# GpSimd's subtractions of weight panels and memory parts, whole or in pieces of 256 columns

## The chip, the core and the metric

The kernel runs on one core of one Trainium2 chip. The time is the device time of one launch in microseconds. Five engines matter: TensorE (PE in the profile), whose weight loads are shown apart (PEld), VectorE (DVE), ScalarE (ACT), GpSimd (POOL) and SyncE (SP), which issues the weight DMAs. Each engine works through its own queue in order and waits for the others by semaphores.

## The reference, cut to what matters

The model is three transformer-like layers over 256 tokens of width 1024: a convolution layer, a layer of differential attention and a layer of mixed sparse attention, the first two each followed by a cross attention over 256 memory tokens, all three with a gated feed-forward block. Nearly all of the work is products of activations with weights that are used once:

```python
k = (mem @ w_k).reshape(B, M, MEM_HEADS, MEM_HEAD_DIM)
v = (mem @ w_v).reshape(B, M, MEM_HEADS, MEM_HEAD_DIM)
...
x = x + swiglu(rms_norm(x, norm_ffn[i]), ffn_w_gate[i], ffn_w_up[i], ffn_w_down[i])
```

All is float32. The kernel keeps the accuracy by splitting each operand a into a high part, which is a rounded to the format that TensorE multiplies in one pass, and a low part, a minus the high part. A product is then hi x hi + hi x lo + lo x hi. The change concerns the subtraction that makes the low parts.

## The kernel before, in words

The weights come as 382 panels of 128 rows and up to 1024 columns, listed in the order of use by `declare`. For each panel `load_to` issues a DMA from SyncE into a buffer `wf` (six of them), and `prep_to` makes the two parts in a ring of five buffers each: ScalarE copies `wf` to `whi` with rounding, and VectorE or GpSimd subtracts, `wlo = wf - whi` (line 278). Which of the two is set per group of panels by a table of letters, `LO`, that is repeated over the panels of the group: "gv" gives every other panel to GpSimd, "g" all of them, "v" none. All panels of the four products for memory K and V (`mk`, `mv`: 4 x 8 panels of 1024 columns) are GpSimd's.

`gemm` consumes panels in order and keeps five prepared ahead. For a panel with `nk` of 1 TensorE multiplies 128 columns of the panel at a time, three products for each, 24 matmuls of 256 columns for 1024 panel columns. A panel with `nk` of 2 or 4 holds several row blocks side by side, so one panel serves 2 or 4 steps. A matmul that reads `wlo` waits for the subtraction that wrote those columns.

Memory parts: the keys and values of the memory are split in the same manner after their product, in quarters of 512 columns (`mem_parts`, line 585): `memK0`, `memV0` and `memV1` on GpSimd, `memK1` on VectorE. The memory itself is split by `mem_split` (line 503), also on GpSimd, which isn't touched.

GpSimd has more in its queue between the panels: sums of squares for the norms (`sacc`, line 338), their folds (`sfold`, line 355), inverse square roots of a few numbers (`rr`, line 372; `orr`, line 918) and the gated products of the last block (`hf`, line 1391). VectorE has, beside its panels, the residuals and low parts of activations, the normalisation of the convolution (`lsq`, line 624), the scaling of attention (`p` in lines 708 and 890, `o` in line 923) and the masked minima (line 324), behind which ScalarE's exponentials `sp` follow. Engine order is fixed when the program is built; at run time only the waits decide.

Of the kernel before, what the change touches and what calls it, by code (L numbers as in the profile page):

```python
# [21 lines left out]
F32 = mybir.dt.float32  # L22
# [3 lines left out]
OP = mybir.AluOpType  # L26
# [157 lines left out]
def program(ctx: ExitStack, tc: tile.TileContext, A, out):  # L184
    nc = tc.nc
    V, SC, G, PE = nc.vector, nc.scalar, nc.gpsimd, nc.tensor
# [69 lines left out]
    def load_to(n):  # L256
        while state["dma"] < min(n, len(panels)):
            p = panels[state["dma"]]
            p["f"] = stage.tile([128, WMAX], F32, name="wf", tag="wf")
            nc.sync.dma_start(p["f"][:, :p["W"]], p["ap"])  # L260
            for f in state["loads"].get(state["dma"], []):
                f()
            state["dma"] += 1

    def prep_to(n):
        while state["prep"] < min(n, len(panels)):
            i = state["prep"]
            load_to(i + 1)
            p = panels[i]
            W = p["W"]  # L270
            p["hi"] = ring.tile([128, WMAX], F32R, name="whi", tag="whi")
            p["lo"] = ring.tile([128, WMAX], F32R, name="wlo", tag="wlo")
            with ExitStack() as late:
                for ins in state["after"]:
                    late.enter_context(tc.issue_after(ins.ins))
                p["ih"] = SC.activation(p["hi"][:, :W], p["f"][:, :W], AF.Copy)  # L276
                eng = G if p["eng"] == "g" else V
                p["il"] = eng.tensor_tensor(p["lo"][:, :W], p["f"][:, :W], p["hi"][:, :W].bitcast(F32), op=OP.subtract)  # L278
            state["prep"] += 1
            load_to(i + NS_PANEL)  # L280

    def consume():
        i = state["use"]
        prep_to(i + state["ahead"])
        state["use"] += 1
        return panels[i]
# [190 lines left out]
    for j in range(4):  # L477
        for c in (2 * j, 2 * j + 1):
            to_set(S0, c, x[:, c], vc("g_mix", c))
        prep_to(j + 1)  # L480
        st.add(x[:, 2 * j:2 * j + 2])
# [99 lines left out]
    def mem_parts(dst, src, n, act, after, eng=G):  # L581
        with tc.issue_after(act.ins):
            SC.activation(dst[0][:, n], src[:, n], AF.Copy)
        with tc.issue_after(after.ins):
            eng.tensor_tensor(dst[1][:, n], src[:, n], dst[0][:, n].bitcast(F32), op=OP.subtract)

    def split(dst, at, ps):
        SC.activation(dst[0][at], ps, AF.Copy)
# [53 lines left out]
    with tc.high_priority():  # L642
        rs = spread(st.r)
        for s in (slice(0, 1), slice(1, 2), slice(2, 4), slice(4, 6), slice(6, 8)):
# [7 lines left out]
    st = Stats()  # L652
    jobs = [(dst, src, n) for dst, src in ((memK[0], fK[0]), (memV[0], fV[0])) for n in range(4)]
    jobs = [lambda d=d, s=s, n=n: mem_parts([quarters(t) for t in d], quarters(s), n, LN["last"], LN["st"].ins) for d, s, n in jobs]
    gemm(8, S1, FM8, resid(st, [(S0, "g_mem", 0)], bias="b_pw2"), hooks={i: jobs[2 * i:2 * i + 2] for i in range(4)},
         tail=TAIL)
# [3 lines left out]
    def mem_attention(i, Sq, So, st, evac):  # L660
        with ExitStack() as es:
            P = es.enter_context(tc_pool(name=f"ma{i}", bufs=3))
            P1 = es.enter_context(tc_pool(name=f"mq{i}", bufs=1))
            if i:
                K = [P1.tile([128, NCH, S], F32R, name=f"memK1{p}") for p in "hl"]
                W = [P1.tile([128, 2, D], F32R, name=f"memV1{p}") for p in "hl"]
                later = [lambda n=n: mem_parts([quarters(t) for t in K], quarters(memK[1][0]), n, st.square, st.low, V)
                         for n in range(4)]
                later += [lambda n=n: mem_parts([quarters(t) for t in W], quarters(memV[1][0]), n, st.square, st.ins)
                          for n in range(4)]  # L670
            else:
                K, W, later = memK[0], memV[0], []
# [680 lines left out]
    gemm(4, [u[:, 4:8] for u in S1], TM4, evO, tail=TAIL)  # L1353
    state["ahead"], state["after"] = NB_PANEL, late[2:]
    prep_to(state["use"] + 4)
    state["after"] = []
    eb.close()
# [79 lines left out]
```

## Time and profile before

| what | value |
|---|---|
| median of 3 runs | 1178.34 us (1177.95 to 1182.44) |
| the profiled execution | 1176.31 us |
| its span (first to last instruction) | 1174.5 us |
| TensorE matmuls busy | 1121.0 us, 95% |
| VectorE busy | 787.4 us, 67% |
| ScalarE busy | 650.7 us, 55% |
| GpSimd busy | 425.3 us, 36% |
| panel subtractions on VectorE, all widths | 251, 319.0 us |
| panel subtractions on GpSimd, all widths | 131, 285.3 us |

[...] An engine that is idle costs nothing as long as no other waits for it.

### The profile page before, as it was taken

The numbers are of one execution on the slowest core, as the hardware profiler recorded it, in microseconds if no ns is written. First come the engines' busy times: TensorE is split into PE (matmuls) and PEld (weight loads), VectorE is DVE, ScalarE is ACT, GpSimd is POOL, SyncE is SP. The second block draws the span as 40 slices with busy tenths as digits, with TensorE's granted clock in tenths as the row PEclk, the third lists the DMA queues.
The fourth block names the chain that finished last, engine by engine and source line by source line (L and its number), as shares of the span: only waits on it lengthen the run. The fifth ranks groups of instructions, "written<-read, shape, count | busy, mean of one in ns | idle before, by whom it ended". The sixth has DMA issues, their size and how long they took to land.

```text
span 1174.5 us, 21545 instructions
## 1 busy us (share of the span) xinstructions
PE 1121.0 (95%) x8418; PEld 1061.5 (90%) x8418; DVE 787.4 (67%) x1445; ACT 650.7 (55%) x1141; POOL 425.3 (36%) x278
## 2 busy tenths in 40 slices
PE   7999989999999998988999999999889998999997
PEld 7998878999999998978999999999887677999986
DVE  6899856586766456666754565645758746888843
ACT  6565476565545354654756554535576645675642
POOL 5999846220000015773626444001554210111300
PEclk9999989999999999998999999999889998999999
DMA  7576534355546544542433654753645115454661
GB/s 259 194 248 211 186 116 170 108 164 188 190 144 232 184 148 145 193 132 84 133 119 129 216 193 143 236 183 105 209 162 163 36 55 163 160 196 155 224 197 37
DMA packets 59799, 191.13 MB, mean 163 GB/s; under 512 B 6752, under 2 KB 10080, under 8 KB 59696
## 3 DMA queue, kind: packets, MB, share of 16 engines
q1 hardware_dynamic: 58288, 187.31, 48.4%
q0 software_dynamic: 688, 1.90, 0.5%
q8 instruction: 66, 1.08, 0.4%
q10 hardware_dynamic: 720, 0.53, 0.1%
q14 instruction: 37, 0.30, 0.1%
HBM read 188.15 MB, written 1.05 MB: 161 GB/s over the span
## 4 chain that ended last, share of the span: by engine, by line
PE 44%; DVE 2%; issue 2%; POOL 1%; ACT 1%; POOLq 0%; DVEq 0%; ACTq 0%
PE acc L409 38%; PE acc L1116 1%; PE acc L1214 1%; DVE wlo L278 1%; POOL sacc L338 1%; PE acc L723 0%; PE acc L1275 0%; PE acc L1279 0%; PE aux L1256 0%; PE acc L1368 0%; POOL sfold L355 0%; PE acc L1276 0%; PE acc L1211 0%; PE acc L692 0%; POOL rmr L1320 0%
## 5 line engine op out<-in xcount | busy, mean ns | idle before, releaser
L276 ACT ACTIVATE whi<-wf 128x1024 fp32r<-128x1024 f32 (+3 forms) x382 | 370.9, 986 | 318.9 <-PE acc L409 277.0
L278 DVE TENSOR_TENSOR wlo<-wf,whi 128x1024 fp32r<-128x1024 f32 (+3 forms) x251 | 319.0, 1280 | 180.5 <-ACT whi L276 179.6
L278 POOL TENSOR_TENSOR wlo<-wf,whi 128x1024 fp32r<-128x1024 f32 (+1 forms) x131 | 285.3, 2194 | 183.5 <-ACT whi L276 183.3
L409 PE MATMUL acc<-s0h,whi 128*128 128x256 f32 x1192 | 340.5, 287 | 5.9 <-ACT whi L276 5.4
L409 PE MATMUL acc<-s0h,wlo 128*128 128x256 f32 x1192 | 338.2, 284 | 3.5 <-POOL wlo L278 3.5
L409 PE MATMUL acc<-s0l,whi 128*128 128x256 f32 x1192 | 337.6, 284 | 1.6 <-DVE s0l L435 1.6
L409 PEld LDWEIGHTS acc<-s0h,whi 128*128 128x128 f32 x1192 | 229.9, 193 | 7.2 <-ACT whi L276 5.4
L409 PEld LDWEIGHTS acc<-s0h,wlo 128*128 128x128 f32 x1192 | 229.1, 192 | 4.9 <-POOL wlo L278 4.6
L409 PEld LDWEIGHTS acc<-s0l,whi 128*128 128x128 f32 x1192 | 229.6, 193 | 1.9 <-DVE s0l L435 1.8
L409 PE MATMUL acc<-s1h,whi 128*128 128x256 f32 x736 | 205.9, 281 | 1.0 <-ACT s1h L649 1.0
L409 PE MATMUL acc<-s1h,wlo 128*128 128x256 f32 x736 | 205.5, 280 | 0.6 <-DVE wlo L278 0.3
L409 PE MATMUL acc<-s1l,whi 128*128 128x256 f32 x736 | 205.5, 280 | 0.3 <-DVE s1l L435 0.3
L409 PEld LDWEIGHTS acc<-s1h,whi 128*128 128x128 f32 x736 | 138.1, 188 | 1.7 <-ACT s1h L649 1.4
L409 PEld LDWEIGHTS acc<-s1h,wlo 128*128 128x128 f32 x736 | 138.3, 188 | 1.0 <-DVE wlo L278 0.5
L409 PEld LDWEIGHTS acc<-s1l,whi 128*128 128x128 f32 x736 | 138.4, 188 | 0.7 <-DVE s1l L435 0.5
L409 PE MATMUL acc<-hh,whi 128*128 128x256 f32 x352 | 99.6, 283 | 0.0
L409 PE MATMUL acc<-hl,whi 128*128 128x256 f32 x352 | 99.6, 283 | 0.0
L409 PE MATMUL acc<-hh,wlo 128*128 128x256 f32 x352 | 99.6, 283 | 0.0
L338 POOL TENSOR_TENSOR sacc<-sq,sacc 128x512 f32<-128x512 f32 x21 | 33.8, 1612 | 122.1 <-ACT sq L337 121.7
L543 DVE SCALAR_TENSOR_TENSOR aux<-u,vecs,aux 128x256 f32<-128x256 f32 x174 | 68.6, 476 | 1.2 <-ACT aux L541 1.2
L409 PEld LDWEIGHTS acc<-hl,whi 128*128 128x128 f32 x352 | 67.6, 192 | 0.0
L409 PEld LDWEIGHTS acc<-hh,wlo 128*128 128x128 f32 x352 | 67.6, 192 | 0.0
(371 smaller groups left out, 1724.6 us busy)
## 6 DMA issues: line engine op xcount, KB each, us to landing
wf<-in_gu SPq DMA_DIRECT2D x120, 512.0 KB, 3.9
wf<-in_w_down SPq DMA_DIRECT2D x66, 512.0 KB, 4.3
wf<-in_mem_w_k SPq DMA_DIRECT2D x16, 512.0 KB, 4.3
wf<-in_mem_w_v SPq DMA_DIRECT2D x16, 512.0 KB, 3.7
wf<-in_mem_w_q SPq DMA_DIRECT2D x16, 512.0 KB, 3.5
wf<-in_mem_w_o SPq DMA_DIRECT2D x16, 512.0 KB, 4.2
wf<-in_w_pw SPq DMA_DIRECT2D x24, 256.0 KB, 3.0
wf<-in_gv SPq DMA_DIRECT2D x24, 256.0 KB, 2.6
```

What stands on the lines that cost most here:

```text
L276: p["ih"] = SC.activation(p["hi"][:, :W], p["f"][:, :W], AF.Copy)
L278: p["il"] = eng.tensor_tensor(p["lo"][:, :W], p["f"][:, :W], p["hi"][:, :W].bitcast(F32), op=OP.subtract)
L338: self.ins = self.eng.tensor_tensor(self.acc, sq, self.acc, op=OP.add)
L409: PE.matmul(o, l, r, start=(ki == 0 and n == 0 and q == 0), stop=(ki == K - 1 and q == 2), skip_group_check=True)
L543: V.scalar_tensor_tensor(cv[:, c] if k == TAPS - 1 else ai, src, w, ai, op0=OP.mult, op1=OP.add)
L1116: PE.matmul(ph[0:60, 0:256], win[:, a, 4 * g + j], w[:, j * 256:(j + 1) * 256], start=(g == 0 and j == 0 and w is p["hi"]), stop=(g == 3 a ...
L1214: PE.matmul(f, q1, kk[:, kv], start=True, stop=True, skip_group_check=True)
```

## The change

Where GpSimd makes a low part, the instruction over the whole width becomes one instruction for each 256 columns: four for a panel of 1024, two for 512, four for 816 (three of 256 and one of 48), two for a quarter of a memory part. VectorE's subtractions stay whole.

```diff
-                eng = G if p["eng"] == "g" else V
-                p["il"] = eng.tensor_tensor(p["lo"][:, :W], p["f"][:, :W], p["hi"][:, :W].bitcast(F32), op=OP.subtract)
+
+                eng, step = (G, 256) if p["eng"] == "g" else (V, W)
+                for c in range(0, W, step):
+                    w = slice(c, min(c + step, W))
+                    p["il"] = eng.tensor_tensor(p["lo"][:, w], p["f"][:, w], p["hi"][:, w].bitcast(F32), op=OP.subtract)
...
         with tc.issue_after(after.ins):
-            eng.tensor_tensor(dst[1][:, n], src[:, n], dst[0][:, n].bitcast(F32), op=OP.subtract)
+            for c in range(0, 512, 256 if eng is G else 512):
+                w = slice(c, c + (256 if eng is G else 512))
+                eng.tensor_tensor(dst[1][:, n, w], src[:, n, w], dst[0][:, n, w].bitcast(F32), op=OP.subtract)
```

The order of instructions on TensorE, VectorE, ScalarE and SyncE stays what it was; GpSimd's has 343 instructions more, and only one panel is taken apart by another instruction. Lines after the edit are 3 to 5 higher than before (278 becomes 281, 338 becomes 341, 918 becomes 923).

That place is the end of the first down projection and the differential attention behind it. GpSimd's queue there before (`sacc` and `sfold` are the norm's sums, `k` is a buffer filled with zeros, `orr` an inverse square root of the attention; x14 counts equal rows):

```order
L827 MEMSET k 64x8x256
L338 TENSOR_TENSOR sacc<-sq,sacc 128x512 x2
L278 TENSOR_TENSOR wlo<-wf,whi 128x1024
L338 TENSOR_TENSOR sacc<-sq,sacc 128x512
L355 TENSOR_TENSOR sfold<-sacc 128x256
L372 TENSOR_TENSOR rr<-ms,mhalf 128x2
L278 TENSOR_TENSOR wlo<-wf,whi 128x1024 x14
L918 TENSOR_TENSOR orr<-oms,mhalf 128x4
L278 TENSOR_TENSOR wlo<-wf,whi 128x1024 x4
```

and now:

```order
L832 MEMSET k 64x8x256
L341 TENSOR_TENSOR sacc<-sq,sacc 128x512 x2
L281 TENSOR_TENSOR wlo<-wf,whi 128x256 x3
L341 TENSOR_TENSOR sacc<-sq,sacc 128x512
L281 TENSOR_TENSOR wlo<-wf,whi 128x256
L358 TENSOR_TENSOR sfold<-sacc 128x256
L375 TENSOR_TENSOR rr<-ms,mhalf 128x2
L281 TENSOR_TENSOR wlo<-wf,whi 128x256 x56
L923 TENSOR_TENSOR orr<-oms,mhalf 128x4
L281 TENSOR_TENSOR wlo<-wf,whi 128x256 x16
```

The last piece of the first panel has moved behind the last `sacc`, ahead of `sfold`; the other panels are four pieces each in the same place.

On TensorE the matmuls stand where they stood, and what moved is a wait. This is the second query product of the first memory attention, whose panel (`whi_2114`, `wlo_2115`) serves four steps of 256 columns, before:

```order
L409 MATMUL acc_2335<-s0h_79,wlo_2115 128x256 [waits Pool_49]
L409 MATMUL acc_2335<-s0h_79,whi_2114 128x256
L409 MATMUL acc_2335<-s0l_80,whi_2114 128x256
L409 MATMUL acc_2335<-s0h_79,wlo_2115 128x256
L409 MATMUL acc_2335<-s0h_79,whi_2114 128x256
L409 MATMUL acc_2335<-s0l_80,whi_2114 128x256
L409 MATMUL acc_2335<-s0h_79,wlo_2115 128x256
```

and now (the same panel is `whi_2261`, `wlo_2262`):

```order
L412 MATMUL acc_2485<-s0h_79,wlo_2262 128x256 [waits Pool_49]
L412 MATMUL acc_2485<-s0h_79,whi_2261 128x256
L412 MATMUL acc_2485<-s0l_80,whi_2261 128x256
L412 MATMUL acc_2485<-s0h_79,wlo_2262 128x256
L412 MATMUL acc_2485<-s0h_79,whi_2261 128x256
L412 MATMUL acc_2485<-s0l_80,whi_2261 128x256
L412 MATMUL acc_2485<-s0h_79,wlo_2262 128x256 [waits Pool_49]
```

The first wait is now for one piece, and the step that reads the next 256 columns has a wait of its own.

## Rows read from the trace of the kernel before

**Rows 1.** The page, busy us of each engine, share of the span, instructions

```profile
PE 1121.0 (95%) x8418; PEld 1061.5 (90%) x8418; DVE 787.4 (67%) x1445; ACT 650.7 (55%) x1141; POOL 425.3 (36%) x278
```

**Rows 2.** Waits of TensorE: waiter, releaser, total us, times, longest us

```profile
PE aux L361 <- POOL sfold L355: 10.5, 7, 2.9
...
PE acc L926 <- DVE o L923: 4.4, 3, 2.0
PE acc L409 <- POOL wlo L278: 3.8, 6, 1.0
...
PE acc L1214 <- ACT sp L1173: 2.9, 1, 2.9
PE aux L712 <- DVE p L708: 2.3, 1, 2.3
...
PE aux L895 <- DVE p L890: 1.9, 1, 1.9
PE aux L630 <- DVE lsq L624: 1.7, 1, 1.7
```

**Rows 3.** Timeline of GpSimd, memory K and V: start us, us, instruction

```profile
115.05 0.64 POOL L612 TENSOR_TENSOR csum<-u,csum 128x256 f32<-128x256 f32 x1
115.65 2.41 POOL L278 TENSOR_TENSOR wlo<-wf,whi 128x1024 fp32r<-128x1024 f32 x1
118.01 0.74 POOL L612 TENSOR_TENSOR csum<-u,csum 128x256 f32<-128x256 f32 x1
118.71 4.77 POOL L278 TENSOR_TENSOR wlo<-wf,whi 128x1024 fp32r<-128x1024 f32 x2
```

**Rows 4.** Chain of waits, second feed-forward block: start us, us, what

```profile
648.17 169.78 PE acc L409 x1440
```

**Rows 5.** Timelines of VectorE and GpSimd, 886 to 899

```profile
888.31 1.20 DVE L278 TENSOR_TENSOR wlo<-wf,whi 128x1024 fp32r<-128x1024 f32 x1
...
890.03 6.08 DVE L278 TENSOR_TENSOR wlo<-wf,whi 128x1024 fp32r<-128x1024 f32 x2
...
888.75 6.29 POOL L278 TENSOR_TENSOR wlo<-wf,whi 128x1024 fp32r<-128x1024 f32 x2 [2.36 <-ACT whi L276]
```

**Rows 6.** Timelines of VectorE and GpSimd, 518 to 530

```profile
521.41 2.94 DVE L923 TENSOR_TENSOR o<-o,orr 128x256 f32<-128x256 f32 x2
...
524.46 2.11 DVE L888 SCALAR_TENSOR_TENSOR dcc<-dcc,lamc,dsm 128x2 f32<-128x2 f32 x1
...
521.24 2.49 POOL L278 TENSOR_TENSOR wlo<-wf,whi 128x1024 fp32r<-128x1024 f32 x1 [0.34 <-ACT whi L276]
524.04 2.52 POOL L278 TENSOR_TENSOR wlo<-wf,whi 128x1024 fp32r<-128x1024 f32 x1 [0.31 <-ACT whi L276]
```

**Rows 7.** Timelines of VectorE and GpSimd, 541 to 552

```profile
543.29 2.33 DVE L919 TENSOR_TENSOR orr<-orr,r 128x4 f32<-128x4 f32 x1 [1.12 <-POOL orr L918]
545.65 2.91 DVE L923 TENSOR_TENSOR o<-o,orr 128x256 f32<-128x256 f32 x2
...
543.22 2.38 POOL L278 TENSOR_TENSOR wlo<-wf,whi 128x1024 fp32r<-128x1024 f32 x1
```

**Rows 8.** Waits of TensorE, 541 to 552

```profile
PE acc L926 <- DVE o L923: 3.1, 2, 2.0
```

**Rows 9.** Timelines of VectorE and GpSimd, 584 to 593

```profile
587.89 2.40 DVE L708 TENSOR_SCALAR p<-p,sm 128x256 f32<-128x256 f32 x2
...
587.52 2.35 POOL L278 TENSOR_TENSOR wlo<-wf,whi 128x1024 fp32r<-128x1024 f32 x1
```

**Rows 10.** Timelines of VectorE and GpSimd, 145 to 202

```profile
147.73 3.26 DVE L624 TENSOR_TENSOR lsq<-lsq 128x512 f32<-128x512 f32 x2 [0.60 <-ACT lsq L622]
...
147.25 2.39 POOL L278 TENSOR_TENSOR wlo<-wf,whi 128x1024 fp32r<-128x1024 f32 x1 [1.69 <-ACT whi L276]
```

**Rows 11.** Timelines of VectorE and GpSimd, 56 to 63

```profile
57.31 2.88 DVE L553 SCALAR_TENSOR_TENSOR u<-t,vecs,sg 128x256 f32<-128x256 f32 x1 [4.66 <-ACT sg L552]
...
54.99 4.91 POOL L278 TENSOR_TENSOR wlo<-wf,whi 128x512 fp32r<-128x512 f32 x3
```

## The prediction

> **What bounds the kernel now.** I read the busy times first. TensorE's matmuls cover 95% of the span and GpSimd only 36% [rows 1], so GpSimd's own busy time is not the limit; the reader should see there that only what TensorE waits for can be won. The second view is therefore the list of TensorE's waits [rows 2]. Its largest entry, `sfold`, comes behind GpSimd sums of squares that the change leaves whole. Six others lead to the low halves: 3.8 us straight for `wlo` of GpSimd, and 4.4, 2.9, 2.3, 1.9 and 1.7 us behind VectorE operations (`o`, the mask chain before `sp`, two kinds of `p`, `lsq`). Together 17.0 us; that is the most which the change can reach by these waits.
>
> The third view, the timelines of VectorE and GpSimd at those five places, shows why VectorE is late there. Two panel subtractions that follow each other take 6.08 us, where the one just before took 1.20 [rows 5]; a GpSimd panel lies across each. Two multiplications `o` take 2.94 us, and a 128x2 operation 2.11 us, each ending as a GpSimd panel ends [rows 6]. So a VectorE operation with two inputs in SBUF stands still until GpSimd's current instruction is done, and a GpSimd instruction is a whole panel of 1024 columns, 2.36 us (the distance of the starts 115.65 and 118.01 in [rows 3]). The reverse is there too: GpSimd's two panels beside the 6.08 us take 6.29 instead of two times 2.36 [rows 5].
>
> [...]
>
> **What a piece costs GpSimd.** The trace has no subtraction of 256 columns. The nearest rows are additions of 256 columns with the next instruction right behind: starts 115.05 to 115.65 and 118.01 to 118.71, so 0.60 and 0.70 us [rows 3]. Four pieces take 2.40 to 2.80 us against 2.36 whole. I take 0.65, so 2.60. The edit adds 99x3 + 31 + 3 + 12 = 343 instructions; at 0.01 to 0.11 us more per piece GpSimd works 5 to 50 us longer over the whole span, nearly all of it in its idle 64%. The one place without idle time is the stretch of memory K and V, 32 panels that are all GpSimd's. TensorE takes 169.78 / 1440 x 24 = 2.83 us per panel [rows 4], so 2.60 keeps ahead by 0.23 and 2.80 just keeps up. The cover ends at 2.83 / 4 = 0.71 us per piece.
>
> [...]
>
> **The terms, each by this rule: VectorE now waits for the rest of one piece, runs, lets one piece pass, and runs again.** That GpSimd gets in between two VectorE operations is what [rows 5] show.
> - *Mask chain near 890* [rows 5]. GpSimd's panel can start at 889.5, when the 1.20 us subtraction ends. First piece to 890.15, subtraction to 891.35, piece to 892.0, subtraction to 893.2, where it was 896.1. That is 2.9 sooner, the whole of TensorE's wait of 2.9. The exponentials behind follow at their own pace; I take **2.5** (bounds 0 and 2.9).
> - *`o` and `p` near 521* [rows 6]. Waiting lasted from 521.41 to 523.73, so the pair itself needs 0.62. New: piece to 521.9, 0.31, piece 0.65, 0.31, so 523.2 instead of 524.35. The 128x2 operation then waits at most one piece, to about 524.1 instead of 526.6, but each of the two operations for `p` behind it can also pay a piece. Bounds 0 and 3.2 (1.9 for `p`, and 4.4 - 3.1 = 1.3 for `o`, the rest being the next term's); I take **1.6**.
> - *`o` near 545* [rows 7]. `orr` waited out a panel, and the pair `o`, 0.62 alone, was done at 548.56. New: piece to 543.87, 0.16, piece 0.65, 0.31, piece 0.65, 0.31, done near 546.0. TensorE waits 3.1 there [rows 8]; **2.5** (bounds 0 and 3.1).
> - *`p` near 588* [rows 9]. The pair took 2.40, of which 1.98 was waiting (to 587.52 + 2.35). New: 0.28 + 0.21 + 0.65 + 0.21 = 1.35, so 1.05 sooner, less 0.25 because four memory parts ahead of it in GpSimd's queue become eight pieces: **0.8** (bounds -0.3 and 2.3).
> - *`lsq` near 148* [rows 10]. 3.26 us for two additions, 1.91 of it waiting. New: 0.17 + 0.68 + 0.65 + 0.68 = 2.18: **1.1** (bounds 0 and 1.7).
> - *TensorE's own waits for `wlo`* [rows 2]. Matmuls now wait for the piece whose columns they read, so the first comes 0.6 to 1.8 us earlier. But where GpSimd works without a break, as before the first 1024-column panel [rows 11], a late panel makes the next one late, so only the last wait of a row counts, and slower pieces take some back: **0.6** (bounds -3 and 3.8).
> - *One reordered panel.* Near the end of the first down projection three pieces go ahead of the last sum of squares and the fourth between it and `sfold`. The work before `sfold` is the same: **-0.2** (0 to -0.4, by 0.60 to 0.70 per piece).
>
> Added waits: 226 more of TensorE's matmuls test a semaphore, nearly always one already passed because panels are prepared five ahead. The extra tests of ScalarE and SyncE name their own earlier `whi`, which is over. I cost them at nothing; the uncovered case is in the second rival.
>
> Sum: 2.5 + 1.6 + 2.5 + 0.8 + 1.1 + 0.6 - 0.2 = 8.9 us. The profiled execution took 1176.31 us (span 1174.5 and 1.8 around it), so 1167.4; it lies 2.0 under the median of 1178.34, and with that the forecast is **1169 us**, its own range 1163 to 1173.
>
> **The rivals.**
> 1. *VectorE does not get in between pieces.* If GpSimd's next piece is in hand when one ends, VectorE waits for the whole panel as before. For it: near 57 an operation took 2.88 us because two GpSimd subtractions that stood in a row passed ahead of it, up to 54.99 + 4.91 = 59.90 [rows 11]. Against: in [rows 5] VectorE got in between two GpSimd panels that stood back to back. Then only the 0.6 and -0.2 are left: 1178.
> 2. *GpSimd pays back.* The same lock lets VectorE hold up every piece, so a panel can lose 1.2 us up to four times instead of once, and chains of short VectorE operations pay a piece each time. If the terms for `o`, `p` and `lsq` come at half (-3.0) and the `wlo` term at -1.4 (-2.0): 8.9 - 5.0 = 3.9, 1174. For it: the 6.29 us in [rows 5]. Against: at the five places VectorE has few two-input operations per panel.
> 3. *Slower: GpSimd becomes the bound in memory K and V.* From 0.71 us per piece TensorE waits in each of the 32 panels. At 0.85 us it is 32 x (3.40 - 2.83) = 18.2 us, and 18.2 - 8.9 = 9.3 more than before: 1188. For it: that stretch leaves GpSimd 0.47 us per panel now (2.83 - 2.36). Against: 0.60 and 0.70 in [rows 3], with that very subtraction next in the queue.
>
> **How the numbers follow.** Within 0.5% is 1172.4 to 1184.2, about what a measurement here can tell from no change. The forecast gets 0.70, rival 1 0.14, rival 2 0.09, rival 3 0.07. Faster is the forecast, 0.70; the same is rivals 1 and 2, 0.23; slower is rival 3, 0.07. For eight in ten, the range goes from 1161 (all 17.0 us gone: 1178.3 - 17.0) to 1179, which takes in rivals 1 and 2.
>
> **What would show it.** Right: VectorE's panel subtractions beside GpSimd stay under 2 us; the pair near 890 ends about 3 us sooner; TensorE's waits for `o`, `sp` and both `p` fall from 11.5 (4.4 + 2.9 + 2.3 + 1.9) to under 5; the mean of GpSimd's pieces is below 0.9 us. Wrong: VectorE operations of 2.4 us remain (rival 1); GpSimd's pieces average over 1 us and new waits for `wlo` or `sfold` appear (rival 2); starts of uncontended pieces lie over 0.71 us apart and TensorE waits for `wlo` between 65 and 140 us (rival 3).

## The result and the profile after

The changed kernel is slower: 1191.72 us (four runs, 1187.17 to 1199.57) beside 1178.14 of the kernel before on the same chip, a ratio of 1.0127 with a 95% interval of 1.0108 to 1.0147. The forecast was 1169. The profiled execution took 1187.17 us (span 1185.4), 10.9 more than that of before. It is the fastest of the four, so what the others lost beyond that has no trace.

Three moments that both traces have show where this lies. TensorE spreads the layer norm's `rr` (L381) at 167.0 us, before at 154.5: 12.5 us are lost until there. Its first transposes of the differential attention stand at 511.9 and 490.7: 8.7 more are lost between. The last matmul ends at 1179.4 and 1168.5, so 10.4 are won behind it. The sum is 12.5 + 8.7 - 10.4 = 10.8. Time was won where four of the forecast's terms lie, and two losses that it did not have were larger.

The first lines are the page's busy times and TensorE's waits after the change (total us, times, longest).

```profile
PE 1120.9 (95%) x8418; PEld 1058.0 (89%) x8418; DVE 792.7 (67%) x1445; ACT 651.9 (55%) x1141; POOL 484.2 (41%) x621
...
PE aux L635 <- DVE lsq L629: 8.6, 1, 8.6
PE acc L412 <- POOL wlo L281: 5.2, 10, 1.2
...
PE acc L412 <- DVE s0l L438: 5.0, 1, 5.0
...
PE aux L900 <- DVE p L895: 4.1, 3, 2.9
...
PE acc L931 <- DVE o L928: 1.6, 2, 1.2
...
PE aux L717 <- DVE p L713: 1.3, 2, 0.9
```

TensorE is as busy as in [rows 1]. Against [rows 2] the wait for `o` fell from 4.4 to 1.6 us, for `p` of the memory attention from 2.3 to 1.3, that for `sp` is gone. `lsq` rose from 1.7 to 8.6, `s0l` from 1.6 to 5.0, and of the 4.1 for `p` L895 a single 2.9 is new. The next lines are the timelines of VectorE and GpSimd at these places. In what follows, a run is a row of GpSimd instructions without idle time between them (a line with a count can be the part of a run in the stretch shown); VectorE is held while a run passes ahead of an operation that it has begun, and gets in when that operation is done between two instructions of the run.

```profile
58.13 7.10 DVE L556 SCALAR_TENSOR_TENSOR u<-t,vecs,sg 128x256 f32<-128x256 f32 x1 [4.75 <-ACT sg L555]
...
56.47 8.47 POOL L281 TENSOR_TENSOR wlo<-wf,whi 128x256 fp32r<-128x256 f32 x12
...
66.58 30.79 POOL L281 TENSOR_TENSOR wlo<-wf,whi 128x256 fp32r<-128x256 f32 x44
...
151.73 11.37 DVE L629 TENSOR_TENSOR lsq<-lsq 128x512 f32<-128x512 f32 x3
...
150.49 12.06 POOL L281 TENSOR_TENSOR wlo<-wf,whi 128x256 fp32r<-128x256 f32 x16
...
198.10 6.37 DVE L281 TENSOR_TENSOR wlo<-wf,whi 128x1024 fp32r<-128x1024 f32 x1
...
197.80 5.59 POOL L281 TENSOR_TENSOR wlo<-wf,whi 128x256 fp32r<-128x256 f32 x8
...
500.53 10.96 DVE L893 SCALAR_TENSOR_TENSOR dcc<-dcc,lamc,dsm 128x2 f32<-128x2 f32 x1
...
499.63 11.84 POOL L281 TENSOR_TENSOR wlo<-wf,whi 128x256 fp32r<-128x256 f32 x17
...
542.99 1.83 DVE L928 TENSOR_TENSOR o<-o,orr 128x256 f32<-128x256 f32 x2
...
562.01 0.69 DVE L924 TENSOR_TENSOR orr<-orr,r 128x4 f32<-128x4 f32 x1 [1.12 <-POOL orr L923]
562.74 1.80 DVE L928 TENSOR_TENSOR o<-o,orr 128x256 f32<-128x256 f32 x2
...
604.76 1.25 DVE L713 TENSOR_SCALAR p<-p,sm 128x256 f32<-128x256 f32 x2
...
895.87 1.26 DVE L281 TENSOR_TENSOR wlo<-wf,whi 128x1024 fp32r<-128x1024 f32 x1
...
893.12 7.45 POOL L281 TENSOR_TENSOR wlo<-wf,whi 128x256 fp32r<-128x256 f32 x9 [0.86 <-ACT whi L276]
```

The lower rows are the forecast's rule at work: a pair of `o` 1.83 and 1.80 us where [rows 6, 7] had 2.94 and 2.91, `orr` 0.69 for 2.33, `p` 1.25 for 2.40 [rows 9], a panel subtraction of the mask chain 1.26 where a pair had 6.08 [rows 5]. The upper rows break it. `dcc`, 128x2 elements, takes 10.96 us and ends at 511.49, just behind the last of 17 pieces (499.63 + 11.84 = 511.47); sixteen pieces passed ahead of it. `wlo` took 6.37 us behind 8 pieces, the first `lsq` 9.1 of its 11.37 behind 13, `u` 7.10 where [rows 11] had 2.88. They came at the 25th (`dcc`), 22nd, 77th and 37th instruction of runs of 40, 29, 91 and 46; before that `wlo` VectorE had got in three times, and the `wlo` came at the 17th instruction after the last of these. So VectorE waits not for a piece but for what is left of the run; only `lsq`, done at 160.83, got in two pieces before the end of its run at 162.55. And 44 pieces in 30.79 us are 0.70 us each, the upper bound taken from [rows 3], 2.80 us a panel.

### The profile page after: what moved, and what is told of

It reads as the page before. It is cut to its first block, busy times and chain, and to the rows that moved or that the text cites. A ratio compares the mean times of both kernels' runs of the same rounds, so it can differ in the third digit from the quotient of the medians.

```text
span 1185.4 us, 21970 instructions
## 1 busy us (share of the span) xinstructions
PE 1120.9 (95%) x8418; PEld 1058.0 (89%) x8418; DVE 792.7 (67%) x1445; ACT 651.9 (55%) x1141; POOL 484.2 (41%) x621
## 4 chain that ended last, share of the span: by engine, by line
PE 43%; POOL 3%; issue 2%; DVE 1%; ACT 1%; POOLq 0%; DVEq 0%; ACTq 0%
PE acc L412 36%; POOL wlo L281 1%; PE acc L1121 1%; POOL sacc L341 1%; PE acc L1219 1%; PE acc L728 0%; PE acc L1280 0%; PE acc L1284 0%; POOL sfold L358 0%; PE aux L1261 0%; PE acc L1373 0%; PE acc L1281 0%; PE acc L1216 0%; PE acc L1202 0%; PE acc L697 0%
## 5 line engine op out<-in xcount | busy, mean ns | idle before, releaser
L281 DVE TENSOR_TENSOR wlo<-wf,whi 128x1024 fp32r<-128x1024 f32 (+3 forms) x251 | 309.9, 1244 | 188.2 <-ACT whi L276 179.1
L281 POOL TENSOR_TENSOR wlo<-wf,whi 128x256 fp32r<-128x256 f32 x462 | 345.0, 789 | 146.0 <-ACT whi L276 145.7
```

The source lines that it names most:

```text
L281: p["il"] = eng.tensor_tensor(p["lo"][:, w], p["f"][:, w], p["hi"][:, w].bitcast(F32), op=OP.subtract)
```

## Experiments

**Where the loss and the gain lie.** `"h"` stands for GpSimd in pieces of 256, `"g"` for whole panels; memory parts are whole in the first two kernels and in that of 512 columns.

```diff
 # e1: pieces from w_o on (and K, V, q, pw1, mq, mo as before)
-o="g", mq1="gvv", mo1="vgv", gu1="gv", T="vvg", cmp="ggv", w="gv", gv2="vgv"
+o="h", mq1="hvv", mo1="vhv", gu1="hv", T="vvh", cmp="hhv", w="hv", gv2="vhv"
 # e2: pieces in these alone
-pw1s="gv", pw1="g", mk="g", mv="g"
+pw1s="hv", pw1="h", mk="h", mv="h"
 # e4: everywhere, but two pieces a panel
-eng, step = (G, 256) ...
+eng, step = (G, 512) ...
```

> Pieces only for the panels of w_o, of the second memory attention and of what follows; every earlier GpSimd panel and every memory part whole again. Theory A (a VectorE instruction with two SBUF operands waits until a whole run of consecutive GpSimd pieces is through; the 10.9 us come from the long runs before 205 us and at 500 us): the long waits (lsq 9.1, wlo 6.4, dcc 11.0 us) are gone and the gains near 545, 588 and 890 us stay, so about 1178.2 - 6 = 1172 us, between 1169 and 1176. Theory B (a piece costs GpSimd 0.70 us and makes it the bound of memory K and V): also below before, 1170 to 1176, since K and V are whole. Theory C (more instructions and semaphores cost time everywhere): half of the pieces are left, so above 1178, near 1183.

Measured: 1167.34 us, ratio 0.9906 (0.9891 to 0.9921), faster than A and B allowed, so it does not tell them apart. Theory C falls: 132 of the 343 new GpSimd instructions (410 in all, before 278) are left, and the kernel is 10.5 us faster than the one before.

> Pieces only for the panels of w_pw1 and of memory K and V (before 160 us) and for the memory parts; all others whole as before. Theory A: the lsq addition near 151 us waits some 9 us again, the first u of a group some 7; 1178.2 + 8 = 1186 us, between 1183 and 1190. Theory B: TensorE's weight waits in 60 to 160 us are there in any case, but they sum to some 5 us; 1183 us with the wait at 151 us no part of it. Theory C: a quarter to a half of the whole loss, 1181 to 1184.

Measured: 1196.36 us (1189.23 to 1204.21), ratio 1.0157 (1.0117 to 1.0196), more than any theory gave. The profile has the `lsq` wait (7.9 us of TensorE) and one that the profile of the changed kernel did not have: `u` at 39.55 us takes 24.16 us, until a run of 42 instructions is through, and TensorE stands still for 12.9. The same operation at 38.97 us of the changed kernel got in, at the 12th instruction of GpSimd's run; here it was held from the 11th on. So the long wait can miss one execution and strike another. That this makes the scatter of the changed kernel's runs is not shown, as only the fastest has a trace.

> GpSimd takes panels in pieces of 512 columns (two for 1024), memory parts whole (512). A piece of 512 was spaced 1.25 us, so a panel costs GpSimd 2.5 us against TensorE's 2.83. Theory A: GpSimd catches up and stops for the next panel, the runs are short, the lsq addition waits under 4 us; the gains are about half of those of 256 columns; 1174 to 1180 us. Theory B: GpSimd is no bound, 1174 to 1178 us. A time above 1184 would speak against both.

Measured: 1173.22 us, ratio 0.9963 (0.9949 to 0.9978). That is 0.8 us below what A and B gave. The first `lsq` took 4.73 us, to the end of a run of 47 instructions, not under 4: GpSimd did not stop for each panel.

**One of VectorE's operands in PSUM.**

```diff
 # e3: first tile in PSUM, last sum in SBUF
-LN[j] = tmp.tile([128, 2, S], F32, name="lsq", tag="sq" if j else "sacc")
+LN[j] = tmp.tile([128, 2, S], F32, name="lsq", tag="sq") if j else b2(aux())
...
-V.tensor_tensor(LN[0], LN[0], LN[j], op=OP.add)
+V.tensor_tensor(to, LN[j], LN[0], op=OP.add)
 # e10: e3 and
-sg = poolC.tile([128, S], F32, name="sg", tag="sg")
+sg = ps[:, S:2 * S]
 # e6: e1 with the edit of e3; e11: e1 with both
```

> All pieces as in the changed kernel, but the sum of squares of the layer norm is kept in PSUM, so that each of its three VectorE additions near 151 us reads one operand from SBUF and one from PSUM instead of two from SBUF (the last writes SBUF). The pieces and their cost stay. Theory A: the u - mean subtractions, which read SBUF and PSUM, ran at 0.64 us each in the middle of the same run of pieces, so the additions run at once (under 1 us each), TensorE's wait at 154 us falls from 8.7 to under 2 us, and the time by 6 to 8 us against the changed kernel, to about 1184. Theory B: the wait is GpSimd's backlog, the weights come no sooner, the time changes by under 2 us (1190 to 1192).

Measured: 1195.81 us, ratio 1.0155 (1.0139 to 1.0171): no gain, and yet not what B said either. TensorE's waits and the timelines of VectorE and GpSimd of this kernel:

```profile
PE acc L412 <- DVE t L553: 12.7, 1, 12.7
...
PE aux L381 <- POOL rr L375: 9.1, 2, 7.0
```

```profile
38.70 23.33 DVE L556 SCALAR_TENSOR_TENSOR u<-t,vecs,sg 128x256 f32<-128x256 f32 x1 [0.18 <-ACT sg L555]
...
164.47 0.69 DVE L630 TENSOR_TENSOR aux<-lsq,aux 128x512 f32<-128x512 f32 x1
...
166.65 0.69 DVE L630 TENSOR_TENSOR lsum<-lsq,aux 128x512 f32<-128x512 f32 x1
...
163.26 11.10 POOL L281 TENSOR_TENSOR wlo<-wf,whi 128x256 fp32r<-128x256 f32 x16
174.29 1.74 POOL L375 TENSOR_TENSOR rr<-ms,mhalf 128x2 f32<-128x2 f32 x1
```

The additions run in 0.69 us in the middle of the pieces, as A said. But the next link, `rr`, is GpSimd's own and stands in its queue behind the same pieces: it starts at 174.29, and TensorE waits 7.0 us for it. Near 150 to 175 us GpSimd's backlog costs TensorE 7.0 us with the hold of `lsq` gone. The long wait of `u` is here too, so this time says nothing on what the hold of `lsq` alone cost; e13 below does.

> Pieces everywhere as in the changed kernel, the layer norm's sum of squares in PSUM, and the sigmoid of the gated unit written to PSUM too, so that neither the additions near 151 us nor the products u near 39, 58 and 91 us read two operands from SBUF. GpSimd's pieces cost the same. Theory A: of the waits before 165 us (TensorE stood still 12.9 us at 61 us in the kernel with the sum in PSUM alone) none over 2 us is left; what is left are the waits of wlo near 169 and 205 us and of the mask operation near 510 us, some 14 us of TensorE; 1195.8 - 12.9 = 1183 us, between 1179 and 1187. Theory B (GpSimd's cost of 0.70 us a piece is the bound there): no change, 1192 to 1197.

Measured: 1204.38 us (1195.12 to 1211.88), ratio 1.0235 (1.0196 to 1.0274). Both expectations missed. The products `u` no longer wait, but a VectorE operation over 128x64 (`lsc`) right behind one waits 20.66 us, and TensorE stands still for 9.2 us at 108 us, behind a `whi`.

> The kernel with pieces only in the panels of w_o and later (1167.3 us) and, with it, the layer norm's sum of squares kept in PSUM. Panels are whole where the additions run. Theory A: the additions no longer wait for a panel, TensorE's wait for the sums near 150 us (1.9 us) falls under 0.6; 1165.5 to 1166.5 us. If the wait only moves to the next VectorE operation, as it did with pieces everywhere: 1167.

Measured: 1164.85 us, ratio 0.9882 (0.9864 to 0.9900), 0.7 below A's range: `lsq` is out of TensorE's waits.

> Pieces only in the panels of w_o and later, with both the sum of squares and the sigmoid in PSUM: the candidate for the best version. Panels are whole where the products u run; they waited up to 3 us for a panel, but TensorE waited under 1 us behind them. Theory A: 1163 to 1165 us, 0 to 1.5 below the kernel with the sum alone (1164.9).

Measured: two groups, 1160.59 and 1163.22, and 1182.43, 1182.88 and 1183.80; the ratio, 0.9872 (0.9846 to 0.9897), is that of the lower group. The median of all five, 1182.43, is above the kernel before on that chip (1176.75), so A missed, and this version can't be called better. The profile is one of the upper, and its timeline shows what happens there, with whole panels:

```profile
59.78 28.21 DVE L511 SCALAR_TENSOR_TENSOR lsc<-memK 128x64 f32<-128x64 f32 x1
...
57.17 30.75 POOL L281 TENSOR_TENSOR wlo<-wf,whi 128x1024 fp32r<-128x1024 f32 x13
```

A 128x64 operation waits 28.21 us, until 57.17 + 30.75 = 87.92, through more than ten panels of 1024. TensorE stands still for 17.1 us at 113 us, behind a `whi`; that this follows from the hold is likely and not shown. So pieces are not needed for the wait, only a run that does not end. The lower group has no trace, so that it differs by this wait isn't shown either.

**The wait by itself.** The probes let GpSimd run subtractions one behind the other and bring VectorE's operation at a chosen place.

> No part of the model is computed: a kernel that measures the disputed wait by itself. In each of 18 trials GpSimd starts a run of subtractions that stand directly behind each other (32 of 256 columns in eight trials, 12 of 1024 columns in six, 32 of 256 in two, and in the last two 16, then one that waits for ScalarE some 2 us, then 24), while VectorE first copies PSUM to PSUM (0.6 us each; 2, 5, 8, 11, 14, 17, 20, 24 copies, then 3, 8, 12, 16, 24, 32, then 20, 20, then 26, 38) and then runs one operation over 512 columns: a subtraction of two SBUF operands; in the first of the two trials with 20 copies one SBUF and one PSUM operand, in the second a copy from SBUF to SBUF. Theory A1 (what decides is how long GpSimd has run without a stop): the two-operand subtraction gets in after one piece when it comes in one of the first 8 pieces, and waits to the end of the run (20, 17, 13, 9, 5 and so on pieces, up to 12 us) from some 12 pieces on; after GpSimd's stop of 2 us it gets in again near the front. With a PSUM operand it runs at once, 0.65 us. Theory A2 (it is chance, or the phase within a piece): waits show no order by the number of copies. Rival theory B (VectorE is held by one GpSimd instruction only): every wait is under 0.8 us for pieces and under 2.5 us for whole panels.

Timelines of VectorE and GpSimd in the first probe: the trial with 11 copies, that with 14, the one with a PSUM operand, the copy from SBUF, and the two behind a stop.

```profile
81.47 1.15 DVE L67 TENSOR_TENSOR two<-vin,two 128x512 f32<-128x512 f32 x1
...
106.41 12.59 DVE L67 TENSOR_TENSOR two<-vin,two 128x512 f32<-128x512 f32 x1
...
379.82 0.68 DVE L67 TENSOR_TENSOR mix<-psa,mix 128x512 f32<-128x512 f32 x1
...
402.10 7.92 DVE L67 COPY one<-vin 128x512 f32<-128x512 f32 x1
...
428.95 0.81 DVE L67 TENSOR_TENSOR two<-vin,two 128x512 f32<-128x512 f32 x1
...
471.14 5.64 DVE L67 TENSOR_TENSOR two<-vin,two 128x512 f32<-128x512 f32 x1
...
73.86 22.30 POOL L67 TENSOR_TENSOR lo<-src,hi 128x256 f32<-128x256 f32 x32
...
96.59 21.85 POOL L67 TENSOR_TENSOR lo<-src,hi 128x256 f32<-128x256 f32 x32
```

A1 holds, with order: behind 2, 5, 8 and 11 copies the operation got in after one piece at most (1.24, 0.78, 1.31, 1.15 us); behind 14, 17, 20 and 24 it waited to the end of the run (12.59, 10.39, 8.18, 5.25). With an operand in PSUM it took 0.68 us at the 21st piece. The copy, with one SBUF operand, waited too. Behind a stop of 5 us it got in at the 4th piece (0.81) and not at the 17th (5.64). The panels of 1024 let it in at every place, up to the 10th of 12.

> Again no part of the model, but the wait by itself, to tell whether the number of GpSimd instructions since its last stop decides, or the time. Runs of 32 subtractions of 256 columns with VectorE's operation behind 11, 12, 13 and 14 copies of 0.73 us (pieces 12 to 15); of 24 of 1024 columns, behind 16, 40, 52 and 64 copies (near panels 5, 13, 16, 20); of 48 of 128 columns behind 4, 8 and 12 (near pieces 7, 13, 20); of 24 of 512 columns behind 10, 18 and 26 (near pieces 6, 11, 15). If the number decides: the operation gets in after one instruction up to about the 12th and waits to the end of the run from about the 14th, whatever the width: whole panels too, 20 us and more at the 13th to 16th. If the time decides (some 8 to 9 us): whole panels would have held it from the 4th on, which the first probe did not show at 22 us, so all panels let it in, pieces of 128 let it in up to the 20th and pieces of 512 hold it from the 7th.

Measured: pieces of 256 held the operation at the 13th, 14th and 15th. The trial with 11 copies was the first and let it in, but at the 17th piece: VectorE's copies before it had got in among its first ones. Pieces of 128 let it in at the 7th, held at the 14th (14.95 us) and the 21st; pieces of 512 let it in at the 6th and 11th, held at the 16th (11.25 us). In time, 128 held 5.4 us into a run and 512 let in at 12.8, so time is not it. But panels of 1024 let it in even at the 20th, against the expectation by number. They wrote the same columns each time, so each waited for the one before, 2.42 us apart.

> The wait by itself once more, no part of the model. First 24 panels of 1024 columns written to five places in turn (so that none waits for the one before it), VectorE's operation behind 16, 40, 52 and 64 copies (near panels 5, 13, 17, 20): if the number of instructions decides, it is held from the 13th on; if whole panels let VectorE in as such, it waits one panel at most. Then 16 pieces of 256 columns and 12 panels, the operation behind 20 and 30 copies (in the 2nd and 5th panel): held to the end by the number. Then 32 pieces that all write the same columns, each waiting for the one before, behind 8 and 20 copies: if a wait for one's predecessor is a stop, let in at both. Last 56 pieces with four operations behind 8, 8, 8 and 16 more copies: if an operation that gets in starts the count anew, the first three get in (at about pieces 9, 18, 27) and the fourth, some 17 pieces later, is held to the end; if only GpSimd's stops count, the second is held already.

VectorE and GpSimd in the third probe: panels to five places, at the 13th and 17th; then pieces that write the same columns, at the 18th; then the four operations of one run.

```profile
90.82 1.56 DVE L68 TENSOR_TENSOR two<-vin,two 128x512 f32<-128x512 f32 x1
...
155.82 18.03 DVE L68 TENSOR_TENSOR two<-vin,two 128x512 f32<-128x512 f32 x1
...
350.13 0.68 DVE L68 TENSOR_TENSOR two<-vin,two 128x512 f32<-128x512 f32 x1
...
367.64 1.30 DVE L68 TENSOR_TENSOR two<-vin,two 128x512 f32<-128x512 f32 x1
...
374.59 0.92 DVE L68 TENSOR_TENSOR two<-vin,two 128x512 f32<-128x512 f32 x1
...
381.17 0.92 DVE L68 TENSOR_TENSOR two<-vin,two 128x512 f32<-128x512 f32 x1
...
393.60 8.67 DVE L68 TENSOR_TENSOR two<-vin,two 128x512 f32<-128x512 f32 x1
...
118.14 55.16 POOL L68 TENSOR_TENSOR ring<-src,hi 128x1024 f32<-128x1024 f32 x24
...
335.91 25.88 POOL L68 TENSOR_TENSOR lo<-src,hi 128x256 f32<-128x256 f32 x32
```

The number decides, for panels too: let in at the 13th, held 18.03 us at the 17th, through 7 more. Sixteen pieces and then panels held it 24.82 us. Pieces that wait for their predecessor stand 25.88 / 32 = 0.81 us apart and let it in with no wait at all. And an operation that gets in starts the count anew: of four in one run those at the 8th, 18th and 27th piece got in, the last, 18 pieces behind the third, was held to the end.

**The run broken in the kernel.**

```diff
 # e7: e1 and pieces for w_q, w_vs        # e8: e1 and these shared
-q="g", V="g"
+q="h", V="h"                              +q="hv", V="hhhv"
 # e15: e1 and pieces in the second memory K and V
 # e12 (from the changed kernel), e13 (with e3), e14 (e6 with it)
-w = slice(c, min(c + step, W))
+w = slice(c - (c == W // 2), min(c + step, W))
 # e17 (from e7), e18 (from the changed kernel)
+w = slice(max(c - 1, 0), min(c + step, W))
```

> The kernel with pieces in the panels of w_o and later, and pieces for the 24 panels of w_q and w_vs as well (a run of 40 pieces near 460 to 490 us). Theory A: a VectorE operation that comes late in that run waits to its end (near 11 us in the changed kernel), TensorE waits 2 to 4 us there, 1169 to 1172 us. Theory B (only memory K and V are too tight for pieces): no loss, 1166 to 1167.5, since GpSimd has time enough here.

Measured: 1173.01 us (1167.0 to 1175.06), ratio 0.9956 (0.9938 to 0.9974), 5.7 more than e1, a little more than A's range. The profile is the fastest run: there `dcc` got in after 2.41 us, at 488.5, when ScalarE had just ended a `whi` (488.51). The other six runs, 1170.69 to 1175.06, have no trace, so what cost them the 5.7 us is not shown.

> As the one before, but every second panel of w_q and every fourth of w_vs goes to VectorE, so that GpSimd's run of pieces is broken before it has 12. Theory A: no VectorE operation waits through more than two pieces there; 1166 to 1168 us. Theory B: the same as the one before within 1 us. Were pieces as such what costs (rather than the length of their run), it would also lose 2 us or more against 1167.3.

Measured: 1171.39 us, ratio 0.9939 (0.9918 to 0.9961). Missed: the run was still 16 pieces long. VectorE's panel, at the 14th, took 2.76 us, to just behind its end, and TensorE waited 2.6 for the `q` behind it. The 4.0 us lost against e1 are also what the third reading had (that pieces as such cost); this run does not tell the two apart.

> Pieces in the panels of w_o and later (1167.3 us), and in those of the second memory K and V (some 111 to 160 us), while w_pw1 and the first memory K and V stay whole, so that GpSimd has its lead when the pieces begin and stops at the end of each panel for TensorE to free a buffer (a panel costs it 2.80 us, TensorE 2.83). Theory A' (held where some 13 instructions stand without a stop): with a stop every 4 pieces the lsq additions wait for less than 4 pieces; 1166 to 1169 us. Theory B (0.70 us a piece is too much in K and V): the same, if 2.80 keeps up; if it does not, TensorE waits for wlo there, 1169 to 1172. If pieces hold VectorE whatever stops there are: lsq waits 9 us, 1174 to 1176.

Measured: 1170.67 us, ratio 0.9933 (0.9917 to 0.9948). Missed by 2 to 5 us: GpSimd did not stop once in 73 instructions (90.0 to 151.1 us), the first `lsq` waited 5.75 us to their end, and TensorE 4.5 instead of the 1.8 of e1. The time lies in B's 1169 to 1172, but B's wait isn't there: TensorE waits 3.5 us for `wlo`, in e1 3.8.

> The changed kernel with one column more: the piece that begins the second half of a panel also writes the last column of the piece before it, so that it must wait until that piece is finished. The pieces, their number and all else stay. In the probe, 24 whole panels that each wrote the same columns as the one before (spaced 2.42 us) let VectorE in at the 20th, whereas pieces without such a wait held it from the 13th on. Theory A' (VectorE is held only where about 13 GpSimd instructions follow each other without a stop, and a wait for one's predecessor is a stop): no VectorE operation waits through more than 4 pieces, the long TensorE waits at 61, 154, 199 and 508 us are gone, and the gains of the pieces stay; the stop costs some 0.1 us a panel, at most 3 us in memory K and V; 1191.7 - 18 to 25 = 1167 to 1174 us. Theory B (GpSimd's time for pieces is the bound in K and V): it gets slower, 1193 to 1197. If such a wait is no stop (the width was it): 1190 to 1197.

Measured: 1190.52 us, ratio 1.0106 (1.0089 to 1.0123): no change. In panels of four pieces the extra column made no pause, the pieces stayed 0.69 us apart, and `dcc` waited 11.08 us. In the panels of two pieces before 61 us it did: every second piece starts 0.81 us behind the one before, and there the `u` that took 7.10 us in the changed kernel got in at once (VectorE, then GpSimd):

```profile
59.04 0.53 DVE L556 SCALAR_TENSOR_TENSOR u<-t,vecs,sg 128x256 f32<-128x256 f32 x1 [7.39 <-ACT sg L555]
...
56.34 5.35 POOL L281 TENSOR_TENSOR wlo<-wf,whi 128x257 fp32r<-128x257 f32 x7
```

> As the one before, with the layer norm's sum of squares kept in PSUM. Theory A': its additions no longer wait at all, 1 to 2 us below the one before. Otherwise as the one before.

Measured: 1186.84 us, ratio 1.0078 (1.0065 to 1.0090). As in e3, `rr` waits in place of `lsq` (6.3 us of TensorE). It differs from e12 in the operand of `lsq` alone, on the same chip, and is 3.7 us faster, more than the 1 to 2 expected.

> Pieces only in the panels of w_o and later, the sum of squares in PSUM (1164.9 us), and the overlapping column in those pieces. No VectorE operation was held long there any more, so theory A' expects no change, 1164 to 1166 us; the added stops cost at most 0.1 us a panel on an engine with time to spare.

Measured: 1162.69 us, ratio 0.9873 (0.9860 to 0.9887), with e6 the best version: beside e6's ratio no change, as A' expected.

> The kernel with pieces for w_q and w_vs as well as from w_o on (1173.0 us), with every piece but a panel's first beginning one column early, so that each waits for the one before it. In the probe, pieces that each wrote the columns of the one before stood 0.80 us apart and let VectorE in at once at the 7th and the 18th. Theory A': if the pieces of a panel now stand 0.75 to 0.80 us apart, VectorE is not held near 490 us, the wait of TensorE there is under 1 us, and the time falls to 1165 to 1169 us. If they stay at 0.69 us, as in the kernel with one overlapping column a panel, nothing changes (1172 to 1174).

Measured: 1175.09 us, ratio 0.9979 (0.9966 to 0.9991). The timeline of VectorE and of GpSimd at the place of `dcc`:

```profile
482.85 0.35 DVE L893 SCALAR_TENSOR_TENSOR dcc<-dcc,lamc,dsm 128x2 f32<-128x2 f32 x1
...
482.44 3.27 POOL L281 TENSOR_TENSOR wlo<-wf,whi 128x257 fp32r<-128x257 f32 x4
```

The pause is there (3.27 / 4 = 0.82 us a piece), and the wait is gone: 0.35 for 10.96 us. The time is not better, 6 to 10 us above what A' gave: slower pieces delay what stands behind them, `sfold` by up to 1.1 us and `o`, for which TensorE waits 3.7 us in all. From the first transposes of the attention (491 us) to the last matmul it takes 674.9 us, in e7 664.6.

> The same in the changed kernel, all pieces. Theory A': no VectorE operation waits through more than two pieces, the four long waits of TensorE before 205 and at 508 us are gone. Theory B gets its own price here: at 0.80 us a piece, 3.1 to 3.2 us a panel, GpSimd is behind TensorE's 2.83 in the 32 panels of memory K and V, 9 to 12 us; together 1176 to 1184 us, with TensorE's waits for wlo spread over 65 to 160 us instead of single ones of 5 us and more. If the spacing stays at 0.69: 1190.

Measured: 1202.90 us, ratio 1.0209 (1.0192 to 1.0226). TensorE's waits:

```profile
PE acc L412 <- POOL wlo L281: 11.3, 17, 2.0
PE aux L381 <- POOL rr L375: 11.0, 3, 9.1
```

Of TensorE's waits of 3.8 us and more none is behind `lsq` or `s0l`, 8.6 and 5.0 us in the changed kernel; so far A' is met. And yet it is the second slowest, 19 us above the upper end of the range: a panel is, by the spacing in e17, 3 x 0.82 + 0.70 = 3.16 us, TensorE needs 2.83 [rows 4], and `rr` waits 9.1 us behind what GpSimd has not yet done. That is theory B's mechanism, at 0.79 us a piece; B's price of 9 to 12 us was too low.

## Why the prediction was wrong

- **The step that failed** is the rule under the terms, "VectorE now waits for the rest of one piece, runs, lets one piece pass, and runs again". It holds while GpSimd has run fewer than about 12 instructions since it last stopped or let VectorE in; in a longer run VectorE waits until the run ends, or nearly so (the probes; `dcc`, `wlo`, `u`, `lsq` above). With four instructions a panel that number is reached in three panels instead of twelve. The forecast had the evidence: [rows 11] is an operation at the 21st instruction of a run of 22, held to its end. It was cited for the first rival, and priced there as a wait "for the whole panel as before", although it had lasted to the end of the run.
- **The places with no term.** `wlo` near 198 us, `dcc` near 500 and `u` were left out, since they cost little before. The 8.7 us between 167 and 512 us are TensorE's waits behind the first two, 3.4 more and 2.9, and 2.4 of its own busy time (329.8 for 327.3, at a mean granted clock of 0.97 for 0.98). The last part is not the hold's: e1, where whole panels stand there, has 331.8.
- **The piece cost**, the second step that failed. Taken 0.65, it was 0.70. "2.80 just keeps up" was right for the weights (waits for `wlo` 5.2 us instead of 3.8) and wrong as a cover: GpSimd lost the 0.47 us a panel in which it had caught up, and ran 91 instructions, 98 to 163 us, without a stop. Then whatever needs it waits, VectorE's `lsq` by the hold (forecast: 1.1 won; measured: 6.9 lost), or, with that taken away, GpSimd's own `rr` (e3, e13, e18). GpSimd is busy for 151.8 of the 167.0 us up to the spreading of `rr`, before for 131.2 of 154.5. With the hold of `lsq` gone 3.7 us came back (e13 beside e12), so by this comparison the greater part of the 12.5 us lies with the backlog rather than with that hold; no run takes the backlog away alone. So the third rival had the place and the sign, but its threshold of 0.71 us and its price per panel were of the wrong kind.
- **What was right.** The terms near 521, 545, 588 and 890 us, 7.4 together: TensorE's waits that they name fell from 11.5 to some 4.1 (1.6 + 1.3 + 4.1 less the new 2.9), and 10.4 us were won behind 512 us. The agreement is in part luck: of the 10.4 only 5.3 are time in which TensorE no longer stands still, since its waits for `sfold` and `win` rose by 1.7 there; the other 5.0 are its own busy time (646.5 us for 651.5, at a mean granted clock of 0.98 for 0.97), which the forecast did not have, and why the clock was higher is not shown. With the pieces at these places alone the time is 1167.34, within the forecast's own range.
- **The second rival**, GpSimd held by VectorE piece by piece, shows only in TensorE's waits for `sfold`, 12.0 us where [rows 2] had 10.5. Its "lock" is what [rows 5] show in both directions: VectorE's pair took 6.08 us beside GpSimd, and GpSimd's two panels 6.29 beside the pair.

In short runs the traces show VectorE held to the end of one GpSimd instruction: the 128x2 operation of [rows 6] took 2.11 us and ended with the panel. In a long run it was held through sixteen, 10.96 us. How many operands lie in SBUF does not by itself tell what is held: the subtraction with one operand in PSUM took 0.68 us, but the copy, whose one operand is in SBUF, 7.92, and the pair `p` of [rows 9], with one tensor operand each, 2.40.

Not settled: what in GpSimd brings about the number (12 let in, 13 held for 256 columns; between 7 and 14, 11 and 16, 13 and 17 for 128, 512 and 1024). In the model it isn't sharp: the same `u` got in at the 12th instruction of a run in the changed kernel and was held at the 12th in e3 and the 11th in e2. Nor is it settled why an operation got in late in a run, `dcc` at the 28th piece in e7, `lsq` two pieces before the end in the changed kernel, `lsc` in e10 with 20 of 90 instructions still to come; and how exactly the 12.5 us divide, since every kernel that ended the hold there also slowed GpSimd or met `rr`. Giving memory panels to VectorE was not tried.

## What to carry to other kernels

Before an engine's work is cut into smaller instructions, ask where that engine never stops: there VectorE's operation did not get in between them but waited for the run (10.96 us through sixteen pieces of 0.70), and the cost per instruction ate the lead that ends the run (2.80 us a panel for 2.36, beside TensorE's 2.83). Cut only where GpSimd has idle time within every dozen instructions (in the probes 12 let VectorE in and 13 held it), and put an operand of VectorE into PSUM where it must run beside GpSimd (0.68 us for 8.18 at the same place) and what follows it does not stand in GpSimd's own queue. Taking the hold away by pauses did not pay by itself: the kernel with them in every panel (e18) has a ratio of 1.0209, the changed kernel 1.0127. Look in the trace of before for one operation that waited past an instruction's end: it shows the rule at a place where it costs nothing yet.

## What the runs showed of the hardware

- VectorE operations with two SBUF operands were held up to 18.03 us (whole panels, e16), 24.82 (mixed, e16) and, in the model, 28.21 (e11), by GpSimd instructions that came after them. Behind 20 copies in e5 the subtraction of two SBUF operands took 8.18 us, the copy from SBUF to SBUF 7.92, the subtraction with one operand in PSUM 0.68.
- GpSimd's subtraction: 0.41 us spacing for 128 columns, 0.68 for 256, 1.22 for 512, 2.30 for 1024 in the probes (e9, e5, e9, e16). A wait for the predecessor in each made 256 columns 0.81 (e16).
- Where GpSimd's pieces stood 0.81 us apart for 0.68 (e16) or 0.82 (e17), VectorE's operation was not held: 0.68 us at the 8th and the 18th piece, and 0.35 for `dcc`. After an operation that got in, the count started anew (8th, 18th, 27th piece of one run let in, e16).
- A matmul of the rounded parts is one record in the trace of before (3 x 352 for the 44 panels of the first two down projections, 24 a panel), 0.118 us behind the last (169.78 / 1440 in [rows 4]); a float32 one is two (six for the three of the layer norm's mean, L617).
